# Layer-modulation products of a two-layer diffusion block: from TensorE to a paced VectorE strand

## The chip, the core and the metric

The kernel runs on one core of one Trainium2 chip. The metric is the device time of one execution in microseconds. Five engines matter: TensorE (PE; its weight loads are listed apart as PEld), VectorE (DVE), ScalarE (ACT), GpSimd (POOL), and SyncE (SP), whose queue issues nearly all transfers. Each engine takes its instructions in the order of its own queue, and semaphores make one engine wait for another.

## What is computed

Two layers of a hybrid attention block over 512 latent and 256 context tokens, 2048 wide, in float32. Ahead of each layer a modulation is worked out from two condition vectors (one for the latent stream, one for the context):

```
sc  = silu(c);  scc = silu(c_ctx)
for l in range(2):
    shift, scale, gate       = split(sc  @ w_ada[l] + b_ada[l], 3)
    shift_c, scale_c, gate_c = split(scc @ w_ada[l] + b_ada[l], 3)
    h  = rms(x,  norm_w[l]) * (1 + scale)   + shift
    hc = rms(xc, norm_w[l]) * (1 + scale_c) + shift_c
    ... one input projection (w_in), three kinds of attention (A, B, C), silu gate ...
    x  = x + gate * merge_out(...)            # w_out
    if l == 0: xc = xc + gate_c * merge_out(...)
```

`w_ada[l]` is 2048 x 6144 float32, 48 MB for each layer. Two vectors are multiplied by it, so its reading is large and its arithmetic small. In layer 1 the context's gate is not used, because the context stream ends there.

## The kernel before

The program is written as strands (Python generators) that a planner, the class `Weaver`, interleaves. It keeps a virtual time and a clock for each engine, books an estimated price for each instruction (`bump`), and lets, at each virtual moment, the ready strand with the lowest priority number go on. `gate` holds a strand back while its engine's booked work, or its own data, is more than `AHEAD` = 1.35 us in front of the virtual time. The result is one fixed order for each engine's queue.

The matrix products are exact to float32 by splitting: each weight tile is loaded into a buffer `ws` (3 of them), ScalarE writes its rounded high part to `wh` (3), VectorE writes the remainder to `wl` (2) by the subtraction at line 234, and TensorE multiplies by high and low parts (line 323). One such pair is called a weight piece here; there are 606, in one order, taken in turn by the strand `main` (priority 6) while the strand `splitter` (priority 2) prepares the next. Line 326 holds the transposes, line 228 ScalarE's copies, `S` is the PSUM area of attention scores, `pt` the transposed probabilities. In groups A and B the attention output passes through `ot` to a multiplication on GpSimd (line 277).

The modulation is made by `ada_blocks`, `ada_finish`, `ada_scale` and `ada_gate`. `ada_blocks` takes blocks of columns of `w_ada`. For each it loads the sixteen 128-row tiles; for each of them TensorE uses the 32 columns of `scT` (the two condition vectors and zeros) as weights and streams the 512 (or 256) columns of `w_ada` (line 722) into one of four 32-partition strips of a PSUM bank. `ada_finish` copies the bank to `tm`, sums the strips by small matmuls with the selector `sel` (line 739), which also turns the row to columns, and adds the bias into `ada`.

Layer 0's shift and scale are made at the start, by `ada_scale(0, 256, "s3", ...)`, in blocks of 256 columns. Three parts remain, each in blocks of 512 columns from a ring `wa` of 4 buffers, in groups of four tiles, as bursts with priority 4:

- layer 0's gate (4 blocks, 64 tiles), spawned after attention group B's jobs;
- layer 1's shift and scale (8 blocks, 128 tiles), spawned by layer 0's jobs before group C;
- layer 1's gate (4 blocks, 64 tiles), spawned at the same place in layer 1.

The gates are wanted by `post_out` (it waits for `ev_gate`), when the output projection of their layer begins; shift and scale of layer 1 by `make_h` at the start of layer 1.

Of the kernel before, what the change touches and what calls it, by code (L numbers as in the profile page):

```python
# [18 lines left out]
OP = mybir.AluOpType  # L19
AX = mybir.AxisListType  # L20

D = 2048
# [3 lines left out]
KT = D // 128  # L26
# [13 lines left out]

CUT = [3, 2]

RES = dict(wa=0, s3=8)


def mmc(n):
# [8 lines left out]
class Event:  # L55
# [4 lines left out]
    def __init__(self):  # L60
        self.t = None
# [73 lines left out]
class Kern:  # L135
    def __init__(self, ctx, tc, t):
        self.ctx, self.tc, self.nc, self.t = ctx, tc, tc.nc, t
        self.w = Weaver()
        self.pools, self.avail, self.half = {}, {}, {}
        self.ndram = 0  # L140
        for tag, shape, n in (("s3", (128, 768), 52), ("ws", (128, 512), 3), ("wh", (128, 512), 3),
                              ("wl", (128, 512), 2), ("tm", (128, 512), 5), ("wa", (128, 512), 4),
                              ("pt", (128, 512), 6), ("ot", (128, 256), 2),
                              ("sm", (128, 32), 16)):
            self.pools[tag] = (ctx.enter_context(tc.tile_pool(name=tag, bufs=n)), shape)
            self.avail[tag] = [0.0] * n
        for tag, shape, n in (("g", (128, 512), 6), ("S", (128, 1024), 1)):
            self.pools[tag] = (ctx.enter_context(tc.tile_pool(name=tag, bufs=n, space=bass.MemoryType.PSUM)), shape)
            self.avail[tag] = [0.0] * n
        for tag, n in (("hl", 3), ("hc", 2), ("ck", 3), ("yk", 4), ("rk", 1)):  # L150
            self.avail[tag] = [0.0] * n
        self.static = ctx.enter_context(tc.tile_pool(name="static", bufs=1))
        self.dram = ctx.enter_context(tc.tile_pool(name="scratch", bufs=1, space=bass.MemoryType.DRAM))
# [445 lines left out]
def body(K):  # L599
    nc, t, w = K.nc, K.t, K.w  # L600
# [4 lines left out]
    K.start(ident, t["k_ident"], 65536)  # L605
    flip = K.st([128, 128], name="flip")
    sel = K.st([128, 2], name="sel")
    maskA = K.st([128, 640], BF16, name="maskA")
    maskB = K.st([128, 384], BF16, name="maskB")
    zero = K.st([128, 256], BF16, name="zero")  # L610
    nc.gpsimd.memset(zero, 0.0)
    scT = K.st([128, KT, 32], name="scT")
    nc.vector.memset(scT, 0.0)
    ada = [K.st([128, 48, 2], name=f"ada{l}") for l in range(2)]
    bT = [K.st([128, 48], name=f"bT{l}") for l in range(2)]
# [69 lines left out]
    ev_c, ev_b, ev_go = Event(), Event(), Event()  # L685

    def ada_blocks(l, blocks, stag, ptag, depth, group):
# [6 lines left out]
        for i in range(0, len(items), group):  # L694
# [4 lines left out]
            while len(pend) < group:  # L699
                while nxt < len(items) and len(pend) < depth and K.free(stag) > RES[stag]:  # L700
                    c_, n_, k_ = items[nxt]
# [9 lines left out]
                if len(pend) >= group:  # L711
                    break
                yield lambda: 0.0 if K.free(stag) > RES[stag] else None
            tiles = [pend.popleft() for _ in now]
# [16 lines left out]
    def ada_finish(l, c0, n, ps, ptag):  # L731
        a = yield from K.get("tm")
        yield from K.act(a[:, :n], ps[:, :n])
        K.put(ptag, ps)
        pt = yield from K.get("g")
        yield from K.sync()
        m = n // 128
        for c in range(m):
            nc.tensor.matmul(pt[:, 2 * c:2 * c + 2], a[:, c * 128:(c + 1) * 128], sel, start=c == 0, stop=c == m - 1,  # L739
                             skip_group_check=True)  # L740
        w.pe(0.05 * m)
        f = c0 // 128
        yield from K.wait(ev_b)
        o = ada[l][:, f:f + m, :]
        yield from K.add(o, pt[:, :2 * m].rearrange("p (c m) -> p c m", m=2),
              bT[l][:, f:f + m, None].to_broadcast([128, m, 2]))
        K.put("g", pt)
        K.put("tm", a)
        k0 = f % KT
        if f < KT:  # L750
            ev = ev_sh
        elif f < 2 * KT:
            yield from K.stt(gsc[l][:, k0:k0 + m, :], o, 1.0, nT[l][:, k0:k0 + m, None].to_broadcast([128, m, 2]),
                             OP.add, OP.mult)
            ev = ev_sc
        else:
            ev = ev_gb
        for k in range(k0, k0 + m):
            K.set(ev[l][k])

    def ada_scale(l, n, stag, ptag, depth, group):
        yield from ada_blocks(l, [(c + o, n) for c in range(0, D, n) for o in (0, D)], stag, ptag, depth, group)

    def ada_gate(l, stag, ptag, depth, group):
        yield from ada_blocks(l, [(2 * D + c, 512) for c in range(0, D, 512)], stag, ptag, depth, group)
        yield from K.wait(*ev_gb[l])
        ps = yield from K.get("g")
        yield from K.sync()
        for m in range(2):
            K.tr(ps[:KT, m * 128:(m + 1) * 128], ada[l][:, 32:48, m])  # L770
        w.pe(0.2)
        g = yield from K.get("tm")
        yield from K.act(g[:KT, :256], ps[:KT, :256])
        K.put("g", ps)
        for m in range(2):
            yield from K.store(gscr[l][m], g[:KT, m * 128:(m + 1) * 128], 8192)
        K.put("tm", g)
        K.set(ev_gate[l])
# [452 lines left out]
    def layer(l):  # L1231
# [14 lines left out]
        J = lambda fn: jobs.append(Call(fn))  # L1246
# [183 lines left out]
        ev_c = {(i, s): Event() for i in range(20) for s in ("lat", "ctx") if s == "lat" or i >= 12 or not last}  # L1430
# [407 lines left out]
        for g in range(4):  # L1838
# [3 lines left out]
                jobs.append(zjob(f))  # L1842
            jobs.append(q_job(GB, "B", range(3 * g, 3 * g + 3), (8 + g,)))
            J(lambda g=g: [attend64(GB, "B", h, g, 4 + h // 2) for h in range(3 * g, 3 * g + 3)] and None)
        if l == 0:
            J(lambda: w.spawn(ada_gate(0, "wa", "g", 4, 4), 4))
        for i in (12, 16):
            jobs.append(chunk(GC, "C", [("c", i + j) for j in range(4)], allt))
        jobs.append(FJob(K, W, COL["kpe"], [(0, 384), (384, 768)], rhs_h, ev_h, post_kpe, stack=True))
# [6 lines left out]
        def free_B():  # L1856
            yield lambda: 0.0 if all(e.t is not None for e in ev_y[:10]) else None
            K.put("s3", ropeB["cs"])

        J(lambda: w.spawn(ada_scale(1, 512, "wa", "g", 4, 4) if l == 0 else ada_gate(1, "wa", "g", 4, 4), 4))  # L1860
        for kind, i in ORDER_C:
            if kind == "q":
                jobs.extend(q_jobs(i))
# [32 lines left out]
    def rpb_prep():  # L1896
        yield from K.wait(ev_c)
        K.side(flip, t["k_flip"])
        for l in range(2):
            p = yield from K.get("tm")  # L1900
            nc.gpsimd.memset(p[:120, :64], 0.0)
            K.side(p[:120, 16:47], t["rpb_a"][l].rearrange("h a b -> (h a) b"))
            yield from K.land()
            K.side(rpb_scr[l], p[:120, :64])
            K.put("tm", p)
        for dst, src in ((maskA, t["k_maskA"]), (maskB, t["k_maskB"])):
            p = yield from K.get("s3")
            n = dst.shape[1]
            K.side(p[:, :n], src)
            yield from K.gate("pool")  # L1910
            nc.gpsimd.tensor_copy(dst, p[:, :n])
            w.bump("pool", 0.9)
            K.put("s3", p)
# [7 lines left out]
    def main():  # L1921
        for j in jobs:
            yield from j.run()
        closed[0] = True
# [3 lines left out]
    w.spawn(K.splitter(), 2)  # L1928
    w.spawn(load_x(), 0)
    w.spawn(rpb_prep(), 1)  # L1930
    w.spawn(ada_scale(0, 256, "s3", "g", 10, 2), 3)
    w.spawn(main(), 6)
    w.spawn(worker(), 2)
    w.spawn(worker(), 2)
# [66 lines left out]
```

## Time and profile before

| | us |
|---|---|
| median of 3 runs | 2972.59 (2969.92 to 2973.67) |
| the profiled execution | 2976.81, span 2975.0 |
| PE busy | 2882.8 (97%) |
| PEld busy | 2706.2 (91%) |
| DVE busy | 1758.5 (59%) |
| ACT busy | 1254.2 (42%) |
| POOL busy | 140.1 (5%) |

The profile gives for each engine the time in which an instruction of it ran. TensorE's matmuls are pipelined, so the distance from the start of one group to the start of the next tells what a group takes of the engine's time better than its duration does. The three bursts of modulation lie at 922 to 1160 us (layer 0's gate), 1160 to 1450 us (layer 1's shift and scale) and 2540 to 2710 us (layer 1's gate). Layer 0's attention groups A and B run up to some 1170 us, group C to some 1510 us, the output projection to some 1700 us.

### The profile page before, as it was taken

What the parts mean: (1) busy time and instruction counts of PE and PEld (TensorE: products, weight loads), DVE (VectorE), ACT (ScalarE), POOL (GpSimd) and SP (SyncE); (2) the same over time, 40 slices, a digit from 0 to 9 for tenths busy, and PEclk for the clock granted to TensorE, in tenths of its full rate; (3) what the DMA queues carried; (4) which work ended last, traced back from release to release, by engine and by line L of the source; (5) the groups of instructions that cost most, each with busy time, mean ns of one, the idle gap of its engine ahead of it and who ended that gap; (6) DMA issues with size and microseconds to landing.
All of it is one profiled execution on the core that took longest, in us unless ns stands there. A gap on an engine that the chain in (4) does not pass through costs nothing.

```text
span 2975.0 us, 56930 instructions
## 1 busy us (share of the span) xinstructions
PE 2882.8 (97%) x21819; PEld 2706.2 (91%) x21819; DVE 1758.5 (59%) x4820; ACT 1254.2 (42%) x2730; POOL 140.1 (5%) x189
## 2 busy tenths in 40 slices
PE   5999999999999999999999999999999999999998
PEld 3689999999999899878999989999998999788998
DVE  5345554637757473867634374655677676578643
ACT  4234333425545452545422273443445455346421
POOL 3000000000100010000000000000000000000000
PEclk9999999999999999999999999999999999999999
DMA  9842222221224555547334333333322214543244
GB/s 253 281 136 81 72 78 76 65 70 49 63 60 127 171 145 157 193 150 237 111 111 124 111 104 82 93 96 91 86 73 66 77 59 129 178 156 118 87 154 127
DMA packets 423633, 349.23 MB, mean 117 GB/s; under 512 B 66276, under 2 KB 370210, under 8 KB 423360
## 3 DMA queue, kind: packets, MB, share of 16 engines
q1 hardware_dynamic: 421488, 344.27, 38.7%
q0 software_dynamic: 1872, 1.32, 0.4%
q8 instruction: 171, 2.80, 0.4%
q14 instruction: 102, 0.84, 0.1%
HBM read 303.97 MB, written 32.08 MB: 113 GB/s over the span
## 4 chain that ended last, share of the span: by engine, by line
PE 88%; DVE 5%; DMA 4%; SPq 1%; ACT 1%; issue 1%; DVEq 0%; ACTq 0%
PE g L323 71%; PE S L323 7%; PE g L326 6%; PE g L722 3%; SPq L293 1%; DMA s<-w_ada 1%; DMA s<-scr 1%; ACT s L228 1%; DVE wl L234 1%; DVE s L234 1%; DVE s L267 1%; DVE pt L234 1%; PE g L739 1%; DVE tm L234 0%; DVE s L256 0%
## 5 line engine op out<-in xcount | busy, mean ns | idle before, releaser
L323 PE MATMUL g<-wh,s 128*128 128x256 f32 (+1 forms) x9000 | 1761.5, 289 | 17.1 <-DVE s L234 7.5
L323 PEld LDWEIGHTS g<-wh,s 128*128 128x128 f32 x9000 | 1445.8, 192 | 54.2 <-issue 31.5
L323 PE MATMUL g<-wl,s 128*128 128x256 f32 (+1 forms) x4500 | 1284.5, 285 | 3.0 <-DVE wl L234 3.0
L323 PEld LDWEIGHTS g<-wl,s 128*128 128x128 f32 x4500 | 862.9, 192 | 5.3 <-DVE wl L234 3.9
L234 DVE TENSOR_TENSOR wl<-ws,wh 128x512 fp32r<-128x512 f32 (+1 forms) x598 | 409.7, 686 | 566.2 <-PE g L323 445.9
L228 ACT ACTIVATE wh<-ws 128x512 fp32r<-128x512 f32 (+2 forms) x606 | 372.0, 615 | 471.8 <-PE g L323 428.2
L323 PE MATMUL g<-s,wh 128*128 128x384 f32 (+1 forms) x1664 | 465.2, 356 | 0.9 <-ACT tm L228 0.9
L228 ACT ACTIVATE s<-s,sm 128x640 f32<-128x640 f32 (+3 forms) x260 | 195.8, 753 | 379.9 <-DVE sm L267 295.4
L323 PEld LDWEIGHTS g<-s,wh 128*128 128x128 f32 x1664 | 304.4, 188 | 21.1 <-ACT tm L228 1.1
L323 PE MATMUL g<-s,wl 128*128 128x384 f32 (+1 forms) x768 | 271.7, 354 | 0.0
L228 ACT ACTIVATE tm<-g 128x512 f32<-128x512 f32 (+4 forms) x324 | 160.7, 517 | 247.6 <-PE g L323 147.5
L234 DVE TENSOR_TENSOR pt<-g,pt 128x512 fp32r<-128x512 f32 (+1 forms) x338 | 196.4, 591 | 92.3 <-ACT pt L228 91.1
L323 PE MATMUL S<-s,s 128*128 128x256 f32 (+2 forms) x1260 | 238.8, 318 | 6.5 <-DVE sm L267 6.1
L326 PE MATMUL g<-ident,s 128*128 128x128 f32 x1520 | 232.7, 277 | 9.8 <-DVE s L234 6.1
L228 ACT ACTIVATE pt<-g 128x512 fp32r<-128x512 f32 (+1 forms) x338 | 168.7, 516 | 155.6 <-PE g L326 149.9
L323 PE MATMUL g<-pt,s 128*128 128x256 f32 (+1 forms) x1348 | 216.7, 286 | 7.4 <-DVE pt L234 4.8
L323 PEld LDWEIGHTS S<-s,s 128*128 128x128 f32 x1260 | 187.2, 190 | 28.6 <-DVE sm L267 12.1
L326 PEld LDWEIGHTS g<-ident,s 128*128 128x128 f32 x1520 | 177.3, 142 | 36.1 <-issue 12.6
L323 PEld LDWEIGHTS g<-pt,s 128*128 128x128 f32 x1348 | 186.5, 192 | 17.6 <-DVE pt L234 7.2
L277 POOL TENSOR_TENSOR s<-ot,s 64x256 f32<-64x256 f32 x100 | 79.3, 794 | 1922.2 <-DVE ot L234 1905.9
L323 PEld LDWEIGHTS g<-s,wl 128*128 128x128 f32 x768 | 144.7, 188 | 9.7 <-DVE wl L234 0.2
L251 DVE TENSOR_SCALAR s<-s,sm 128x640 f32<-128x640 f32 (+3 forms) x260 | 131.8, 507 | 6.1
(146 smaller groups left out, 2129.9 us busy)
## 6 DMA issues: line engine op xcount, KB each, us to landing
wa<-w_ada SPq DMA_DIRECT2D x256, 256.0 KB
ws<-w_in SPq DMA_DIRECT2D x328, 128.0 KB
ws<-w_in SPq DMA_DIRECT2D x160, 256.0 KB
ws<-w_out SPq DMA_DIRECT2D x136, 256.0 KB
s<-w_ada SPq DMA_DIRECT2D x128, 256.0 KB
s<-scr SPq DMA_DIRECT2D x36, 384.0 KB
ws<-w_in SPq DMA_DIRECT2D x64, 192.0 KB
ws<-w_qb SPq DMA_DIRECT2D x54, 192.0 KB
```

The costliest lines, as they stand in the source:

```text
L228: self.nc.scalar.activation(out, in_, func, bias=bias, scale=scale, **kw)
L234: self.nc.vector.tensor_tensor(out, a, b, op=op)
L251: self.nc.vector.tensor_scalar(out, a, s1, s2, op0=op0, op1=op1)
L267: self.nc.vector.tensor_tensor_reduce(out, a, b, -1.0, init, OP.add, OP.min, acc)
L277: self.nc.gpsimd.tensor_tensor(out, a, b, op=OP.mult)
L293: self.nc.sync.dma_start(out, in_)
L323: self.nc.tensor.matmul(out, l, r, start=start, stop=stop, skip_group_check=True)
L326: self.nc.tensor.transpose(out, in_, self.ident)
L722: nc.tensor.matmul(ps[j:j + 32, :n], scT[:, kk, :], s[:, x * n:(x + 1) * n], start=kk < 4, stop=kk >= 12, skip_group_check=True)
L739: nc.tensor.matmul(pt[:, 2 * c:2 * c + 2], a[:, c * 128:(c + 1) * 128], sel, start=c == 0, stop=c == m - 1, skip_group_check=True)
```

## The change

Everything behind layer 0's shift and scale is moved from the bursts to one strand, `ada_rest`, with priority 5, spawned when layer 0's shift and scale are done: layer 0's gate, then layer 1's shift and scale, then layer 1's gate. In it, `ada_vec` keeps one accumulator of 128 x 512 for each side (latent, context) in the new pool `ac` (2 buffers; `wa` goes from 4 to 2). For each tile of `w_ada` VectorE multiplies by the tile's column of `scT` and adds into the accumulator: `tensor_scalar` for the first tile of a block, `scalar_tensor_tensor` for the other fifteen. After each tile the strand is held until 4.0 us (`PACE`) of virtual time later. When a block is complete, TensorE sums the accumulator over the partitions by four matmuls for each side with a column of ones (`one`). Layer 1's gate is made for the latent side alone. The selector matmuls of layer 0's shift and scale are booked at 0.21 us instead of 0.05.

```diff
-RES = dict(wa=0, s3=8)
+RES = dict(s3=8)
+PACE = 4.0
...
-("wa", (128, 512), 4),
+("wa", (128, 512), 2), ("ac", (128, 512), 2),
...
+    one = K.st([128, 1], name="one")
+    nc.vector.memset(one, 1.0)
...
-        w.pe(0.05 * m)
+        w.pe(0.21 * m)
+        K.put("tm", a)
+        yield from ada_use(l, c0, n, pt, (0, 1))
+
+    def ada_vec(l, c0s, sides):
+        n = 512
+        items = [(c0, k) for c0 in c0s for k in range(KT)]
+        pend = deque()
+        nxt = 0
+        for c0 in c0s:
+            acc = []
+            for k in range(KT):
+                while nxt < len(items) and (not pend or K.free("wa")):
+                    w.cur.ft = w.vt
+                    s = yield from K.get("wa")
+                    c_, k_ = items[nxt]
+                    nxt += 1
+                    ts = yield from K.load_ahead(s, t["w_ada"][l, k_ * 128:(k_ + 1) * 128, c_:c_ + n])
+                    pend.append((s, ts))
+                s, ts = pend.popleft()
+                yield from K.wait(ev_c)
+                w.cur.ft = max(w.vt, ts)
+                if k == 0:
+                    for _ in sides:
+                        acc.append((yield from K.get("ac")))
+                for a, m in zip(acc, sides):
+                    sc = scT[:, k, m:m + 1]
+                    if k == 0:
+                        yield from K.ts(a, s, sc, OP.mult, fast=True)
+                    else:
+                        yield from K.stt(a, s, sc, a, OP.mult, OP.add)
+                K.put("wa", s)
+                yield w.vt + PACE
+            pt = yield from K.get("g")
+            yield from K.sync()
+            for c in range(n // 128):
+                for a, m in zip(acc, sides):
+                    nc.tensor.matmul(pt[:, 2 * c + m:2 * c + m + 1], a[:, c * 128:(c + 1) * 128], one,
...
+            w.pe(0.21 * n // 128 * len(sides))
+            K.put("ac", *acc)
+            w.spawn(ada_use(l, c0, n, pt, sides), 1, w.cur.ft)
...
-    def ada_gate(l, stag, ptag, depth, group):
-        yield from ada_blocks(l, [(2 * D + c, 512) for c in range(0, D, 512)], stag, ptag, depth, group)
+    def ada_gate(l):
+        sides = (0, 1) if l == 0 else (0,)
+        yield from ada_vec(l, [2 * D + c for c in range(0, D, 512)], sides)
...
-        if l == 0:
-            J(lambda: w.spawn(ada_gate(0, "wa", "g", 4, 4), 4))
...
-        J(lambda: w.spawn(ada_scale(1, 512, "wa", "g", 4, 4) if l == 0 else ada_gate(1, "wa", "g", 4, 4), 4))
...
-    w.spawn(ada_scale(0, 256, "s3", "g", 10, 2), 3)
+    def modulation():
+        yield from ada_scale(0, 256, "s3", "g", 10, 2)
+        w.spawn(ada_rest(), 5)
+
+    def ada_rest():
+        yield from ada_gate(0)
+        yield from ada_vec(1, [c + o for c in range(0, D, 512) for o in (0, D)], (0, 1))
+        yield from ada_gate(1)
+
+    w.spawn(modulation(), 3)
```

Because the planner orders everything anew, the change moves instructions on all engines. In the listings that follow, a row is a line, an operation, its output and inputs; the kernel's lines shift by two in the changed one (234 becomes 236, 256 becomes 258, 323 becomes 325).

TensorE's queue in attention group B of layer 0, kernel before: the first burst's first group of four tiles (`wa,scT`) stands between products with probabilities (`pt`) and the next scores (`S`).

```order
L323 MATMUL g<-pt,s_9235 128x256 x4
L323 MATMUL g<-pt,s_9235 128x128 x2
L722 MATMUL g<-wa,scT 32x512 x4
L323 MATMUL S<-s_9231,s_10412 128x256
L323 MATMUL S<-s_9232,s_10412 128x256
```

In the changed kernel no such group stands between them. TensorE's queue in attention group A of layer 0, changed kernel: the sum of the first block's two accumulators (`ac`) over the partitions, in the midst of a product of the input projection.

```order
L325 MATMUL g<-s_1264,wl 128x384
L325 MATMUL g<-s_1265,wh 128x384
L784 MATMUL g<-one,ac 128x1 x8
L325 MATMUL g<-s_1032,wh 128x384
L325 MATMUL g<-s_1032,wl 128x384
```

On TensorE 64 groups of four rows at line 722 and 64 matmuls at line 739 are gone, and 112 matmuls of one column have come.

VectorE's queue from the 128th weight piece to the 129th (`wl<-ws,wh`), in attention group B of layer 0, kernel before (`ISA` rows are the maxima and the reads of their accumulators, `ot` the attention's output).

```order
L234 TENSOR_TENSOR wl<-ws,wh 128x512
L234 TENSOR_TENSOR sm<-sm 128x1
L272 RECIPROCAL sm<-sm 128x1
L251 TENSOR_SCALAR s_10729<-s_10729,sm 128x640
L267 ISA s_10688,sm<-S,maskB,nsink 128x384
L267 ISA sm 128x1
L234 TENSOR_TENSOR s_10413<-g,s_10413 64x512
L267 ISA s_10688,sm<-S,zero,sm 128x256
L267 ISA sm 128x1
L234 TENSOR_TENSOR pt<-g,pt 128x512
L234 TENSOR_TENSOR sm<-sm 128x1
L234 TENSOR_TENSOR wl<-ws,wh 128x512
```

Everything between the two subtractions belongs to attention. The same stretch of VectorE's queue, the 128th weight piece to the 129th, in the changed kernel.

```order
L236 TENSOR_TENSOR wl<-ws,wh 128x512
L253 TENSOR_SCALAR s_10181<-s_10181,sm 128x512
L258 SCALAR_TENSOR_TENSOR s_9819<-g,colA,s_9818 64x256
L236 TENSOR_TENSOR ot<-g,ot 64x256
L258 SCALAR_TENSOR_TENSOR ac<-wa,scT,ac 128x512 x2
L269 ISA s_10362,sm<-S,zero,nsink 128x256
L269 ISA sm 128x1
L236 TENSOR_TENSOR pt<-g,pt 128x512 x2
L236 TENSOR_TENSOR sm<-sm 128x1
L236 TENSOR_TENSOR wl<-ws,wh 128x512
```

Two accumulations stand between two subtractions that TensorE's weights need, and the attention's work around them is that of another head.

SyncE's queue where the first burst's tiles are issued, kernel before: four tiles of `w_ada` together between weight loads.

```order
L293 DMA ws<-w_in 128x2x256 x4
L293 DMA wa<-w_ada 128x512 x4
L293 DMA ws<-w_in 128x2x256 x2
L293 DMA wa<-w_ada 128x512 x4
L293 DMA ws<-w_in 128x2x256
L293 DMA wa<-w_ada 128x512 x4
```

The changed kernel has no groups of four. SyncE's queue in the changed kernel, in attention group B of layer 0.

```order
L295 DMA wa<-w_ada 128x512
L295 DMA ws<-w_in 128x2x192
L295 DMA ws<-w_in 128x2x64
L295 DMA scr_146<-s_5988 128x768
L295 DMA wa<-w_ada 128x512
L295 DMA ws<-w_in 128x2x192
L295 DMA ws<-w_in 128x2x64
```

The 256 loads of `wa` remain, singly spread from layer 0's group A to its output projection.

## Rows read from the trace of the kernel before

**Rows 1.** The page: busy time by engine, and the chain that ended last by engine.
```profile
PE 2882.8 (97%) x21819; PEld 2706.2 (91%) x21819; DVE 1758.5 (59%) x4820; ACT 1254.2 (42%) x2730; POOL 140.1 (5%) x189
...
PE 88%; DVE 5%; DMA 4%; SPq 1%; ACT 1%; issue 1%; DVEq 0%; ACTq 0%
```

**Rows 2.** Timeline of PE at two places: start us, duration us, engine, line, operation.
```profile
921.82 0.89 PE L323 MATMUL g<-pt,s 128*128 128x256 f32 x6
922.64 1.06 PE L722 MATMUL g<-wa,scT 128*32 128x512 f32 x8
923.63 0.51 PE L323 MATMUL S<-s,s 128*128 128x256 f32 x2
...
953.13 1.05 PE L739 MATMUL g<-sel,tm 128*128 128x2 f32 x8
954.04 0.41 PE L326 MATMUL g<-ident,tm 128*128 128x128 f32 x2
```

**Rows 3.** Timeline of PEld at the first place; in brackets idle time before, and releaser.
```profile
922.63 0.16 PEld L722 LDWEIGHTS g<-wa,scT 128*32 128x32 f32 x8
923.63 0.30 PEld L323 LDWEIGHTS S<-s,s 128*128 128x128 f32 x2 [0.84 <-issue]
```

**Rows 4.** Busy time of each engine in three stretches, columns in the first line.
```profile
core 0: us, PE busy (x) PEld busy (x) DVE busy (x) ACT busy (x) POOL busy (x), PEclk, DMA share, GB/s
203.00:1170.00 967.00, 960.51 (x7241) 936.65 (x7239) 564.38 (x1657) 411.22 (x946) 66.04 (x86) 1.00 0.32 90
1170.00:1511.00 341.00, 332.99 (x2435) 288.43 (x2436) 240.00 (x689) 169.41 (x378) 4.34 (x7) 0.99 0.52 171
2540.00:2710.00 170.00, 164.48 (x1098) 137.61 (x1097) 114.16 (x310) 81.57 (x190) 0.00 (x0) 1.00 0.50 160
```

**Rows 5.** PE and PEld busy time of lines 722 and 739 in the bursts, summed.
```profile
sum 700.00, PE 75.81 PEld 11.82; mean PE 25.27 PEld 3.94
...
sum 1478.00, PE 15.31 PEld 15.86; mean PE 5.10 PEld 5.29
```

**Rows 6.** VectorE's groups by form: count, busy us, mean ns of one, idle before.
```profile
L256 DVE SCALAR_TENSOR_TENSOR s<-s,qaT,s 128x512 fp32r<-128x512 f32 x6 | 4.4, 748 | 1.0 <-ACT s L228 1.0
L256 DVE SCALAR_TENSOR_TENSOR s<-tm,g 128x512 f32<-128x512 f32 x16 | 10.9, 683 | 1.0 <-ACT tm L228 0.2
L251 DVE TENSOR_SCALAR s<-s,gsc,ada 128x512 f32<-128x512 f32 x16 | 8.7, 543 | 0.3
L234 DVE TENSOR_TENSOR wl<-ws,wh 128x512 fp32r<-128x512 f32 x544 | 380.0, 699 | 544.5 <-PE g L323 427.7 <-issue 60.5 <-ACT wh L228 29.9
```

**Rows 7.** What VectorE waits for at `wl`, 203 to 1170 us and 1170 to 1511 us.
```profile
DVE wl L234 <- PE g L323: 139.5, 60, 5.4
...
DVE wl L234 <- PE g L323: 9.4, 8, 3.6
```

**Rows 8.** Seven stretches of 50 us with VectorE fullest: last, and sum.
```profile
2700.00:2750.00 50.00, 48.81 (x379) 47.10 (x378) 44.55 (x123) 33.85 (x81) 0.00 (x0) 1.00 0.31 103
sum 350.00, PE 344.98 PEld 320.53 DVE 287.36 ACT 194.95 POOL 23.59; mean PE 49.28 PEld 45.79 DVE 41.05 ACT 27.85 POOL 3.37
```

**Rows 9.** What PE's weight loads at line 722 wait for, 920 to 2710 us.
```profile
PEld g L722 <- issue: 6.4, 30, 0.3
PEld g L722 <- DMA wa<-w_ada: 5.5, 11, 1.0
PEld g L722 <- DVE s L256: 0.7, 1, 0.7
```

**Rows 10.** Timeline of DVE and of POOL around 278 us.
```profile
277.80 1.24 DVE L234 TENSOR_TENSOR wl<-ws,wh 128x512 fp32r<-128x512 f32 x1
...
277.76 0.73 POOL L277 TENSOR_TENSOR s<-ot,s 64x256 f32<-64x256 f32 x1 [29.55 <-DVE ot L234]
```

**Rows 11.** What SyncE's queue waits for before it issues, the longest entry.
```profile
SPq L293 <- DVE wl L234: 1103.6, 374, 12.0
```

More of the change, by code (lines that the diff above doesn't have):

```diff
@@ L141, in __init__ @@
         for tag, shape, n in (("s3", (128, 768), 52), ("ws", (128, 512), 3), ("wh", (128, 512), 3),
-                              ("wl", (128, 512), 2), ("tm", (128, 512), 5), ("wa", (128, 512), 4),
+                              ("wl", (128, 512), 2), ("tm", (128, 512), 5), ("wa", (128, 512), 2), ("ac", (128, 512), 2),
                               ("pt", (128, 512), 6), ("ot", (128, 256), 2),
@@ L740, in ada_finish @@
                              skip_group_check=True)
-        w.pe(0.05 * m)
+        w.pe(0.21 * m)
[35 more added lines that the diff above has]
+                    nc.tensor.matmul(pt[:, 2 * c + m:2 * c + m + 1], a[:, c * 128:(c + 1) * 128], one,
+                                     start=c == 0 and m == sides[0], stop=c == n // 128 - 1 and m == sides[-1],
+                                     skip_group_check=True)
+            w.pe(0.21 * n // 128 * len(sides))
+            K.put("ac", *acc)
+            w.spawn(ada_use(l, c0, n, pt, sides), 1, w.cur.ft)
@@ L742, in ada_finish, with ada_use @@
+    def ada_use(l, c0, n, pt, sides):
+        m = n // 128
         f = c0 // 128
         yield from K.wait(ev_b)
-        o = ada[l][:, f:f + m, :]
-        yield from K.add(o, pt[:, :2 * m].rearrange("p (c m) -> p c m", m=2),
-              bT[l][:, f:f + m, None].to_broadcast([128, m, 2]))
+        x, y = sides[0], sides[-1] + 1
+        o = ada[l][:, f:f + m, x:y]
+        yield from K.add(o, pt[:, :2 * m].rearrange("p (c m) -> p c m", m=2)[:, :, x:y],
+              bT[l][:, f:f + m, None].to_broadcast([128, m, y - x]))
@@ L747, in ada_finish @@
         K.put("g", pt)
-        K.put("tm", a)
         k0 = f % KT
@@ L768, in ada_gate @@
         yield from K.sync()
-        for m in range(2):
+        for m in sides:
             K.tr(ps[:KT, m * 128:(m + 1) * 128], ada[l][:, 32:48, m])
@@ L772, in ada_gate @@
         g = yield from K.get("tm")
-        yield from K.act(g[:KT, :256], ps[:KT, :256])
+        yield from K.act(g[:KT, :128 * len(sides)], ps[:KT, :128 * len(sides)])
         K.put("g", ps)
-        for m in range(2):
+        for m in sides:
             yield from K.store(gscr[l][m], g[:KT, m * 128:(m + 1) * 128], 8192)
```

## The prediction

> **What bounds the kernel now.** I read busy times and chain first: TensorE is busy 97% of the span and holds 88% of the chain, VectorE is busy 59% and holds 5% of the chain [rows 1]. So TensorE's own work sets the time, and an instruction taken off it is worth what it keeps the next one from starting. Then I read the timeline at a modulation group: the eight records of four tiles (each matmul of this float32 kind has two) start at 922.64 and the next product at 923.63 [rows 2]; the reader is to look at starts, since the printed durations overlap. Last I read the stretches in which the new VectorE work will stand: attention groups A and B of layer 0, 203 to 1170 us, with VectorE busy 564.38 of 967 and TensorE idle 6.5; group C of layer 0, 1170 to 1511 us, with VectorE busy 240.00 of 341 and TensorE idle 8.0 [rows 4]. They tell whether there is room.
>
> The profiled execution took 2976.81 us (span 2975.0 and 1.8 around it), 4.2 above the median of the three runs, 2972.59. The sum below is made against 2976.8, and 4.2 is taken off at the end.
>
> **What TensorE loses and gains.** Removed: 64 groups of four tiles at 923.63 - 922.64 = 0.99 us, 63.4 us. All of it is path, since in both places the engine goes straight on with other work. The busy time of line 722, 75.81 us [rows 5], is the upper end; it counts tails that overlap. Removed too: 64 selector matmuls. Four of them, eight records, take 954.04 - 953.13 = 0.91 us [rows 2], 0.228 each, 14.6 us. Added: 112 matmuls with the column of ones (32 for layer 0's gate, 64 for layer 1's shift and scale, 16 for layer 1's gate), with the same 128 x 128 weights as the selector's, so 0.228 each, 25.5 us. Net: 63.4 + 14.6 - 25.5 = **52.5 us less** on TensorE. The copies of banks by ScalarE and a 16-row transpose that also go are off the path or under 1 us, and I cost them at nothing, as ScalarE is busy 42% [rows 1].
>
> TensorE's waits at the bursts go as well: 5.5 us for tiles, 0.7 for VectorE, 6.4 of issue [rows 9]. Between 0 and 12.6 us; some of that time becomes another wait, since the instruction behind would often not have been ready earlier. I take 4.
>
> **What VectorE gets.** 28 tensor-scalar of 128 x 512 and 420 scalar-tensor-tensor of 128 x 512. The nearest row for the first is 543 ns. For the second there are 748 ns (two SBUF inputs and a per-partition scalar, the same shape, six times) and 683 ns (one input in PSUM) [rows 6]; I take 748, which has the same operands. 28 x 0.543 + 420 x 0.748 = 329 us (302 by 683 ns). VectorE then stands at some 1758.5 + 329 = 2088 us, about 71% of a shorter span.
>
> Where they stand I read from the order, with the 606 weight pieces as a common clock: of the 448, 11 are in front of piece 20, 352 between pieces 20 and 200 (203 to 1170 us in the trace), 64 between 200 and 260 (1170 to 1511 us), 21 behind.
> - Groups A and B: 564 + 352 x 0.748 = 827 us of work in a stretch that stays near 967 us on TensorE (16 groups of tiles and 16 selector matmuls go, -19.5 us; some 11 sums of 1.82 come, +20): 85%. There is slack of the right kind: VectorE stands 139.5 us there waiting for TensorE to free a weight buffer [rows 7], that is, it is early. What does 85% cost TensorE? In the seven 50 us stretches of the trace with the fullest VectorE (41.05 of 50 on average) TensorE is idle 50 - 49.28 = 0.72 us [rows 8], against 6.5/967 x 50 = 0.34 here. 967/50 x 0.38 = 7.3; I take **+8 us**, with 0 and 16 as ends (1.19 in the fullest stretch).
> - Group C: 240 + 64 x 0.748 = 288 us of work. TensorE's own time falls by 32 groups and 32 selector matmuls, 39 us, and two sums come, 4 us: 341 - 35 = 306 us. VectorE would stand at 94%, more than any 50 us of the trace shows (44.55, 89% [rows 8]). And it is early there for only 9.4 us [rows 7]: most of its gaps wait for ScalarE's half of softmax. At 89% the stretch needs 288/0.89 = 323 us, so 17 of the 35 us are given back; at 94% none. I take **+12**.
>
> Such an added instruction also waits for its tile at the head of VectorE's queue, and behind it stand the subtractions for `wl`, for which TensorE waits two pieces later. The ring has only two buffers, but the tile is issued about one tile ahead, and the 4 us of pacing is far over the 0.99 us that four tiles took of TensorE. The 256 loads are the same in number and size; the 16 DMA engines are busy 32% at 203 to 1170 us with 90 GB/s [rows 4], and 176 loads of 256 kB there instead of 64 add some 30 GB/s, which keeps them under half. SyncE's queue now meets a load of `wa` that waits for VectorE between weight loads; but it already waits 1103.6 us for `wl` subtractions in total [rows 11], which means that weights are issued as early as buffers allow. Cost nothing while VectorE keeps up; if it doesn't, that is rival 1.
>
> A wider VectorE share also meets GpSimd. A 128 x 512 subtraction that began 0.04 us after a GpSimd multiplication took 1.24 us, against 0.699 on average [rows 10, 6]. 93 GpSimd operations stand between 203 and 1511 us; with the added work filling 27% of that time, some 25 meet one, 25 x 0.55 = 14 us more of VectorE time and 1 point of its share, inside the ends above. The Trainium skill, "SBUF — State Buffer", section "SBUF: two separate sides", says that a VectorE operation with two SBUF inputs and a GpSimd operation exclude each other for the whole of an instruction; the trace agrees (1.24 us is 0.69 and most of the other's 0.73), and by that rule alone the added work would lose these 14 us, not more.
>
> Behind piece 300 nothing is added. In layer 1 the gate's burst goes: 16 groups, 4 sums of 0.91 for 4 of as much, -16 us, already in the 52.5. VectorE is busy 114.16 of 170 there [rows 4], so it can follow.
>
> **Sum.** 2976.8 - 52.5 - 4 + 8 + 12 = 2940.3 for a profiled execution, less 4.2: **2936 us**, 1.2% less.
>
> **Rival 1, slower: VectorE's queue becomes what TensorE waits for.** Place: groups A to C of layer 0. Each added operation stands in front of softmax and of subtractions in an engine that takes its queue in order; where VectorE is behind the plan, the whole of it is delay for TensorE, and the `wa` load in SyncE's queue holds the weights behind it. It decides from 56.5/329 = 17% of the added time on the path. For it: group C's 94%, and that the planner books 0.60 us for a subtraction that takes 0.699 [rows 6], so it sees free time that isn't there. Against it: 0.72 us idle at 82% [rows 8]. With a third of the added time on the path, 329/3 = 110 us: 2976.8 - 56.5 + 110 - 4.2 = **3026 us**. Chance 0.14.
>
> **Rival 2: full giving back in group C and in the fullest part of group B.** VectorE at no more than 82% on average, what the seven fullest stretches show [rows 8]: group C needs 288/0.82 = 351 us against 306, +45, and A and B 827/0.82 = 1009 against 967, +42. Then 2976.8 - 56.5 + 87 - 4.2 = 3003; with group C alone 2976.8 - 56.5 + 8 + 45 - 4.2 = **2969**, within 0.2% of before. Chance of about that: 0.10.
>
> **Rival 3: TensorE is bound by its weight loads, not by what streams.** Then removing groups with small weights frees only 11.82 us and the selectors' 15.86 [rows 5], and the sums cost 224 records x 15.86/128 = 27.8: nothing is gained, and with +20 for VectorE the time is 2972.6 + 20 = 2993. Against it: behind the group's loads PEld stands idle 0.84 us, and the next load starts with the next product at 923.63 [rows 3]; the streaming holds everything. Chance 0.02. The Trainium skill, "Perfetto Trace Analysis", section "Identifying the Most-Contended Engine", wants TensorE judged by LDWEIGHTS busy share and not by matmul busy time; here the row on PEld speaks against taking it so.
>
> That the change does not do what it says: the last accumulation of layer 0's gate stands, by the order, where the trace has some 520 us and `post_out` asks at 1511; layer 1's scale stands at some 1250 us and is asked for at 1690. No wait can arise there, and I give it nothing.
>
> **How the numbers follow.** My forecast has 0.74, rival 1 0.14, rival 2 0.10, rival 3 0.02. The forecast's own range: the low end takes all waits and none of VectorE's costs, 2976.8 - 52.5 - 12.6 - 4.2 = 2908; the high end takes 16 and 17 and no waits, 2953. Holding 8 in 10 it must take in rival 2, and the first part of rival 1 (where it decides, 2973 and a little over), so 2908 to 2980. About 0.2%, 6 us, is what a measurement of this kernel can tell from no change. Faster by more than that (under 2966.6): 0.74 and a part of rival 2, 0.75. Within: 0.10. Slower: 0.15.
>
> **What would show it.** Right: no line 722 behind 200 us; TensorE's busy time down by 50 to 60 us; VectorE's up by 300 to 340 with the accumulation near 0.75 us; the waits of `wl` for TensorE in groups A and B shorter by about as much as the added work; group C's stretch shorter by 15 to 35 us, layer 1's last 400 us by some 16. Wrong: accumulations of 0.9 us or more, TensorE idle by over 1.5 us in 50 in groups A and B, weight loads (PEld) waiting for `wl`, or SyncE's queue waiting for accumulations while `ws` is wanted.

## The result and the profile after

The changed kernel takes 2958.74 us (median of 4 runs, 2956.14 to 2960.64), the kernel before, measured beside it, 2973.13. The ratio is 0.9949, with a 95% interval of 0.9932 to 0.9967: 0.5% faster, some 15 us, where 36.5 were forecast. The direction was right, the size was not half of it. A repeat on another chip gave 0.9946 (below).

The page of the changed kernel, busy time by engine and the chain that ended last, to be held against [rows 1]:

```profile
PE 2835.2 (96%) x21402; PEld 2716.2 (92%) x21402; DVE 2025.2 (69%) x5269; ACT 1243.4 (42%) x2714; POOL 147.3 (5%) x189
...
PE 77%; DVE 13%; DMA 5%; issue 2%; SPq 2%; ACT 1%; DVEq 0%; ACTq 0%
```

TensorE lost 47.6 us of busy time, near the forecast, but the chain tells that VectorE now holds 13% of what ended last instead of 5%. The span fell by 20.6 in the profiled execution, which is the fastest of its four runs; the medians are 14.4 apart.

With the weight pieces as common clock (VectorE's subtractions for `wl` or `wh` numbers 20, 200 and 260, counted from 0, start at 200, 1189 and 1509 us now, at 203, 1170 and 1511 before) the stretches of the changed kernel are, in the columns of [rows 4]:

```profile
0.00:200.00 200.00, 158.75 (x1333) 119.35 (x1334) 95.20 (x229) 71.60 (x140) 25.57 (x44) 0.99 0.84 249
200.00:1189.00 989.00, 971.05 (x7264) 957.09 (x7264) 783.95 (x2021) 410.44 (x945) 74.03 (x86) 0.99 0.41 117
1189.00:1509.00 320.00, 295.67 (x2146) 280.22 (x2145) 269.31 (x746) 163.10 (x371) 4.28 (x7) 0.99 0.39 122
1509.00:2954.00 1445.00, 1409.76 (x10665) 1359.53 (x10663) 876.75 (x2276) 598.26 (x1260) 43.43 (x52) 0.99 0.35 100
```

| stretch (pieces) | before, us | after, us | difference | forecast |
|---|---|---|---|---|
| start (to 20) | 203 | 200 | -3 | 0 |
| groups A and B of layer 0 (20 to 200) | 967 | 989 | +22 | +8.5 |
| group C of layer 0 (200 to 260) | 341 | 320 | -21 | -23 |
| behind it | 1464 | 1445 | -19 | -16 |

The forecast's column holds 30.5 of its 36.5 us: the 4 us of waits were placed in no stretch, and 2 us of small matmuls behind group C were not counted (see the section on why the prediction was wrong). The profiled execution took 2956.14 us where the sum had 2940.3 for it. So most of the 15.8 us that are missing, 13.5, lie in groups A and B. There TensorE's idle time went from 6.5 us [rows 4] to 989 - 971.05 = 17.95. The rest is the clock. Two stretches of 50 us in groups A and B and two in group C, changed kernel, same columns:

```profile
550.00:600.00 50.00, 45.26 (x307) 43.47 (x307) 42.82 (x124) 22.26 (x55) 3.57 (x5) 0.97 0.33 96
750.00:800.00 50.00, 40.58 (x258) 35.71 (x258) 44.72 (x122) 26.98 (x70) 5.13 (x6) 0.86 0.26 78
1250.00:1300.00 50.00, 41.67 (x283) 37.30 (x282) 43.91 (x128) 24.56 (x56) 0.00 (x0) 0.97 0.25 81
1350.00:1400.00 50.00, 47.94 (x353) 46.76 (x352) 45.84 (x152) 30.86 (x74) 1.06 (x2) 0.97 0.46 139
```

The kernel before had VectorE at 39.84 of 50 in its own 750 to 800 us, and lost nothing of the clock there:

```profile
750.00:800.00 50.00, 47.91 (x319) 46.46 (x319) 39.84 (x131) 27.02 (x73) 5.28 (x7) 1.00 0.25 66
```

From 750 to 800 us TensorE now stands for 9.4 us, and the granted clock averages 0.86 of 2.4 GHz, that is, 14 us of the 50 at the level of 1.2 GHz. With 0.97 from 550 to 600 us the clock cost (0.14 + 0.03) x 50 = 8.5 us. So groups A and B: 11.5 of idle time + 8.5 of clock + 0.5 of added matmuls = 20.5 of the 22.

The last row of the table hides a loss. The output projection of layer 0, before and then changed:

```profile
1511.00:1688.00 177.00, 172.88 (x1440) 172.53 (x1439) 68.07 (x115) 35.44 (x55) 0.00 (x0) 1.00 0.37 114
...
1509.00:1692.00 183.00, 177.38 (x1455) 176.76 (x1454) 81.48 (x138) 35.13 (x56) 0.00 (x0) 0.98 0.47 141
```

It takes 6 us more, with a granted clock of 0.98 instead of 1.00 and 1.5 us more of idle time. The stretch of layer 1's gate takes 23 less (below).

What TensorE waits for from 500 to 1000 us (engine, line, releaser: us in total, times, longest), and an excerpt of its timeline there:

```profile
PE g L328 <- DVE s L253: 5.9, 7, 1.6
PE g L325 <- DVE pt L236: 3.7, 8, 0.8
PE S L325 <- DVE sm L269: 3.1, 7, 0.6
```

```profile
776.42 0.74 PE L325 MATMUL S<-s,s 128*128 128x256 f32 x4 [0.54 <-DVE sm L269]
777.00 0.28 PE L328 MATMUL g<-ident,s 128*128 128x128 f32 x1
778.36 0.90 PE L328 MATMUL g<-ident,s 128*128 128x128 f32 x3 [1.08 <-DVE s L253]
779.90 1.44 PE L325 MATMUL S<-s,s 128*128 128x384 f32 x4 [0.64 <-DVE sm L269]
...
786.49 0.90 PE L328 MATMUL g<-ident,s 128*128 128x128 f32 x3 [1.62 <-DVE s L253]
```

The waits are for softmax: the maximum (line 269), the scaling of the probabilities ahead of their transposes (253), the second half of the transposed probabilities (236). The weight subtraction, which the prediction had named beside softmax, is not among them here. In group C it is the longest entry, for matmuls as for weight loads (1180 to 1500 us):

```profile
PE g L325 <- DVE wl L236: 5.9, 8, 1.9
...
PEld g L325 <- DVE wl L236: 9.0, 11, 2.1
```

And most of the slack I counted on is gone: in groups A and B VectorE waited 139.5 us at `wl` for TensorE [rows 7], now 20.4. Another 68.4 us in front of `wl` (16.2 before) are put down to no engine:

```profile
DVE wl L236 <- issue: 68.4, 48, 3.4
DVE wl L236 <- PE g L325: 20.4, 19, 2.9
```

The added operations by form (count, busy us, mean ns):

```profile
L258 DVE SCALAR_TENSOR_TENSOR ac<-wa,scT,ac 128x512 f32<-128x512 f32 x420 | 308.9, 755 | 9.4 <-DMA wa<-w_ada 8.7
L251 DVE TENSOR_SCALAR ac<-wa,scT 128x512 f32<-128x512 f32 x28 | 13.1, 480 | 5.5 <-DMA wa<-w_ada 4.4 <-PE g L784 1.1
```

### The profile page after: what moved, and what is told of

Its sections match the earlier page's. It is cut to its first block, busy times and chain, and to the rows that moved or that the text cites. A ratio compares the mean times of both kernels' runs of the same rounds, so it can differ in the third digit from the quotient of the medians.

```text
span 2954.4 us, 56418 instructions
## 1 busy us (share of the span) xinstructions
PE 2835.2 (96%) x21402; PEld 2716.2 (92%) x21402; DVE 2025.2 (69%) x5269; ACT 1243.4 (42%) x2714; POOL 147.3 (5%) x189
## 4 chain that ended last, share of the span: by engine, by line
PE 77%; DVE 13%; DMA 5%; issue 2%; SPq 2%; ACT 1%; DVEq 0%; ACTq 0%
PE g L325 65%; PE g L328 5%; PE S L325 5%; DVE s L236 2%; DVE s L269 2%; DVE wl L236 2%; DVE ac L258 2%; SPq L295 2%; DMA s<-w_ada 1%; DMA s<-scr 1%; DVE pt L236 1%; DVE tm L236 1%; DVE s L253 1%; ACT s L230 1%; DVE s L258 1%
## 5 line engine op out<-in xcount | busy, mean ns | idle before, releaser
L258 DVE SCALAR_TENSOR_TENSOR ac<-wa,scT,ac 128x512 f32<-128x512 f32 x420 | 308.9, 755 | 9.4 <-DMA wa<-w_ada 8.7
L230 ACT ACTIVATE tm<-g 128x512 f32<-128x512 f32 (+3 forms) x308 | 150.9, 512 | 247.5 <-PE g L325 139.2
L325 PE MATMUL g<-pt,s 128*128 128x256 f32 (+1 forms) x1348 | 223.8, 290 | 14.9 <-DVE pt L236 8.8
L325 PEld LDWEIGHTS S<-s,s 128*128 128x128 f32 x1260 | 189.3, 192 | 26.2 <-DVE sm L269 15.8
L279 POOL TENSOR_TENSOR s<-ot,s 64x256 f32<-64x256 f32 x100 | 86.7, 867 | 1934.9 <-DVE ot L236 1714.9
```

Of the source, the lines that this page charges most:

```text
L230: self.nc.scalar.activation(out, in_, func, bias=bias, scale=scale, **kw)
L258: self.nc.vector.scalar_tensor_tensor(out, a, s, b, op0=op0, op1=op1)
L279: self.nc.gpsimd.tensor_tensor(out, a, b, op=OP.mult)
L325: self.nc.tensor.matmul(out, l, r, start=start, stop=stop, skip_group_check=True)
```

## The experiments

Two theories at the start. **V**: VectorE's added time takes the gain, through TensorE's waits for softmax and the clock lost behind them. **O**: it is not the time but what came with it, the new order of all queues or the 256 single loads in SyncE's queue.

**The changed kernel again**, on another chip.

> The changed kernel as it is, on the chip of the other runs of this set: 2956 to 2962 us, so that the distances to it rest on the same chip.

Measured 2958.09 us, ratio 0.9946 (0.9934 to 0.9958).

**VectorE's time taken away, order kept.**

```diff
-yield from K.stt(a, s, sc, a, OP.mult, OP.add)
+yield from K.gate("dve")
+nc.vector.scalar_tensor_tensor(a[:, :32], s[:, :32], sc, a[:, :32], op0=OP.mult, op1=OP.add)
+w.bump("dve", 0.07 + 0.06 + 0.00104 * n)
```

> The changed kernel with its order, loads, sums and booked prices untouched, but each of the 420 accumulations works on 32 of its 512 columns (so the modulation behind layer 0's shift and scale is only partly computed). This takes VectorE's time away and nothing else. Theory V (VectorE's added time is what ate the gain, by TensorE's waits and the clock lost behind them): the accumulation falls from 755 ns to about 0.25 us, some 210 us of VectorE time go, and nearly the whole expected gain appears: 2916 us, between 2905 and 2925. Rival O (the new order itself, or the single loads in SyncE's queue): nothing moves, 2950 to 2960.

Measured 2936.69 us, ratio 0.9869 (0.9856 to 0.9883): between the two. The accumulation fell to 256 ns, 209 us of VectorE time went, and 22 us of the kernel's time with it. Some 21 were still missing to the 2916 us of the sum. Every queue had the same order as in the changed kernel, so these can't be VectorE's added time, beyond what the narrow accumulations still take. Its accumulations, and its stretches (pieces 20 to 200, 200 to 260, and behind):

```profile
L778 DVE SCALAR_TENSOR_TENSOR ac<-wa,scT,ac 128x32 f32<-128x32 f32 x420 | 99.9, 256 | 7.5 <-DMA wa<-w_ada 6.8
...
203.00:1178.00 975.00, 964.37 (x7267) 954.51 (x7266) 629.92 (x2021) 410.80 (x946) 65.94 (x86) 0.99 0.41 119
1178.00:1493.00 315.00, 296.32 (x2146) 284.01 (x2146) 241.75 (x747) 162.82 (x371) 4.32 (x7) 0.97 0.40 125
1493.00:2938.00 1445.00, 1409.22 (x10666) 1358.19 (x10665) 865.02 (x2276) 597.63 (x1260) 43.70 (x52) 0.99 0.34 100
```

In group C TensorE still stands for 18.7 us, with hardly more VectorE work than before (241.75 us against 240.00 [rows 4]). So V is true in part, and O in part.

**The same, with nothing booked for the accumulations**, which orders the other work as if they did not exist.

```diff
-w.bump("dve", 0.07 + 0.06 + 0.00104 * n)
+w.bump("dve", 0.0)
```

> As e1_narrow (accumulations on 32 of 512 columns, the modulation behind layer 0's shift and scale only partly computed), and the planner books nothing for them, so that the other work is ordered as if they didn't exist. It tells apart the two reasons why e1_narrow stayed 21 us over what the sum allows. Theory P (the booked load made the planner delay attention's work, and the order carries that): 2913 to 2925 us. Theory F (TensorE's bursts had stood where TensorE would wait anyway, above all in group C, so that taking them out is worth less than their length): 2928 to 2940 us, with TensorE idle over 12 us in pieces 220 to 260.

Measured 2910.31 us, ratio 0.9786 (0.9773 to 0.9799). That is some 64 us, more than the 56.5 I had summed for TensorE, and a little under the range of theory P; in a new order theory F is out. The 256 single loads, the sums on TensorE and 113 us of VectorE work are all in it. So no cost of the loads shows; what was left of theory O is the order that booking the accumulations gave. By the stretches of the two kernels it cost 7 us in groups A and B, 12 in group C (TensorE idle 18.7 us instead of 9.4) and 8 behind it:

```profile
202.00:1170.00 968.00, 960.33 (x7273) 951.12 (x7271) 633.83 (x2048) 409.87 (x942) 65.83 (x86) 1.00 0.43 124
1170.00:1473.00 303.00, 293.64 (x2150) 283.08 (x2151) 240.45 (x739) 162.85 (x373) 4.28 (x7) 0.98 0.42 133
1473.00:2910.00 1437.00, 1404.97 (x10649) 1354.04 (x10648) 861.69 (x2253) 597.72 (x1259) 44.05 (x52) 0.99 0.34 97
```

**The fourth corner: nothing booked, but the accumulations done in full.**

> The full accumulations, but booked at nothing: the order of e5_free on every engine, with VectorE's real time in it. The fourth corner of the square (booked or not, done or not). If the two costs add, order 26 us (e1_narrow less e5_free) and VectorE's real time 22 us (the changed kernel less e1_narrow): 2932 us, 2927 to 2938. If the booking is what keeps VectorE's real time harmless, that is, unplanned work does more harm than planned work: 2945 us or more.

Measured 2972.21 us, ratio 0.9997 (0.9986 to 1.0008). The costs don't add. In this order VectorE's real time (757 ns for an accumulation, against 264) costs 62 us, three times what it costs in the booked order. Its groups A and B:

```profile
202.00:1217.00 1015.00, 978.86 (x7273) 958.65 (x7272) 800.26 (x2048) 409.48 (x942) 74.91 (x86) 0.99 0.41 118
```

VectorE is busy 79% of it, as in the changed kernel (783.95 of 989); TensorE is idle 36.1 us instead of 17.95. The square, by ratios to the kernel before:

| | accumulations of 32 columns | of 512 columns |
|---|---|---|
| booked | 0.9869 | 0.9949 |
| not booked | 0.9786 | 0.9997 |

By these ratios booking costs 25 us of order when VectorE is light, and saves 14 when it is not. What it is in the booked order that TensorE loses to is not shown.

**What a group on TensorE is worth in a fixed order.** Kernel before, every queue as it was, three of four groups in each block narrowed.

```diff
-nc.tensor.matmul(ps[j:j + 32, :n], scT[:, kk, :], s[:, x * n:(x + 1) * n], start=kk < 4, stop=kk >= 12,
+m = 32 if stag == "wa" and kk >= 4 else n
+nc.tensor.matmul(ps[j:j + 32, :m], scT[:, kk, :], s[:, x * n:x * n + m], start=kk < 4, stop=kk >= 12,
```

> The kernel before, order and booked prices untouched, but in the bursts the matmuls of the second to fourth group of each block stream 32 of 512 columns (the modulation behind layer 0's shift and scale is only partly computed). 48 of the 64 groups shrink from 0.99 us to an estimated 0.25. No VectorE work, no new order. If the whole length of a group is path, as my sum has it: 35 us less, 2940 us (2935 to 2945), half of it in pieces 200 to 260. Theory F: pieces 200 to 260 give less than 9 us of their 18, the two gates their 9 each, in all 2948 to 2956 us.

Measured 2954.53 us, ratio 0.9932 (0.9919 to 0.9946), some 20 us, as theory F has it in all. A narrowed group takes 0.20 us from start to start, so 48 x 0.79 = 38 us were taken away (9.5 for each gate, 19 in group C). Timeline of PE at two of them:

```profile
928.10 0.27 PE L723 MATMUL g<-wa,scT 128*32 128x32 f32 x8
928.30 0.74 PE L323 MATMUL S<-s,s 128*128 128x256 f32 x4
...
935.71 0.27 PE L723 MATMUL g<-wa,scT 128*32 128x32 f32 x8
936.42 0.86 PE L323 MATMUL S<-s,s 128*128 128x384 f32 x4 [0.44 <-DVE sm L267]
```

At the second the next product was not ready, and 0.44 us go into a wait for VectorE. Its stretches:

```profile
199.00:1163.00 964.00, 954.17 (x7246) 937.82 (x7246) 565.11 (x1658) 410.98 (x946) 65.98 (x86) 1.00 0.32 90
1163.00:1496.00 333.00, 319.24 (x2436) 293.83 (x2435) 238.69 (x688) 168.40 (x378) 4.34 (x7) 0.98 0.53 176
1496.00:2958.00 1462.00, 1426.53 (x10813) 1368.25 (x10811) 864.83 (x2257) 599.87 (x1264) 43.44 (x52) 0.99 0.36 106
```

The gains are 3, 8 and 2 us. So theory F, which gave the gates their whole 9 us each and the loss to group C alone, has the total but not the place. This profiled execution is the slowest of the five, and in it some 21 of the 38 us came back: TensorE's idle time is 101.2 us instead of 92.2, and its granted clock 0.990 instead of 0.994 on average, 12 us over 2958. In a fixed order about half of what leaves TensorE is given back in this way; with a new order, as above, nothing is.

**Sparser pace.** PACE 5.0 and 6.0 for 4.0.

> The changed kernel with PACE 5.0 instead of 4.0: pieces 20 to 200 hold 286 added operations instead of 353, and some 40 move to layer 1, where VectorE has room. Theory V: the fuller stretches of groups A and B lose less, 2945 to 2953 us. Rival O: no change beyond 3 us, 2956 to 2962, or slower if the last parts come late.

> The changed kernel with PACE 6.0: 246 operations instead of 353 in pieces 20 to 200, layer 1's shift and scale complete only as layer 0 ends. Theory V: 4 to 8 us better than PACE 5.0 up to piece 260, 2940 to 2946, unless layer 1's start waits for the last blocks: then pieces 300 to 320 are longer by 5 us or more, and the whole is 2946 to 2955.

Measured 2947.02 us, ratio 0.9908 (0.9895 to 0.9922), and **2930.06 us, ratio 0.9854 (0.9841 to 0.9868)**: the direction of theory V, with more at the second step than its 2940 to 2946. How much of that is VectorE's time, the next runs tell. PACE 6.0 is the fastest complete kernel of this study, faster than the kernel before and the changed one. Pieces 20 to 200 of it:

```profile
205.00:1164.00 959.00, 953.62 (x7211) 945.14 (x7210) 718.80 (x1913) 411.26 (x944) 70.82 (x86) 1.00 0.37 107
```

VectorE at 75%, TensorE idle 5.4 us, no clock lost: 30 us less than the changed kernel needs there.

**PACE 6.0 without booking, and PACE 6.0 with narrow accumulations.**

> The full accumulations, booked at nothing, PACE 6.0. If both remedies add (sparser pace takes 28 us off the booked kernel, about two thirds of what booking and real time cost together): 2918 to 2926 us, better than each alone. If unplanned work does harm: 2935 or more, worse than PACE 6.0 with booking (2930).

> PACE 6.0 with booking, accumulations on 32 of 512 columns (the modulation behind layer 0's shift and scale only partly computed): what VectorE's real time costs at the sparser pace. If the cost grows with how full VectorE is, much less than the 22 us at PACE 4.0: 2920 to 2928, 2 to 10 under PACE 6.0 with full accumulations. If it goes with the number of operations alone, which is the same: 2908, 22 under.

Measured 2973.41 us, ratio 0.9994 (0.9986 to 1.0003), and 2919.11 us, ratio 0.9813 (0.9798 to 0.9828). Without booking nothing is gained at the sparser pace either. Pieces 20 to 200 of that kernel:

```profile
202.00:1199.00 997.00, 967.68 (x7218) 950.63 (x7218) 739.04 (x1938) 407.72 (x942) 74.72 (x86) 1.00 0.37 106
```

VectorE is busy 74% here, the share of the kernel above, and TensorE idle 29.3 us instead of 5.4. So the share of VectorE alone does not set the cost. With booking, VectorE's real time costs 11 us at this pace (2930.06 less 2919.11), half of the 22 at PACE 4.0, for the same number of operations; the run came out an us under the range of the theory that the cost grows with how full VectorE is. The two kernels with narrow accumulations differ too, 2936.69 and 2919.11, or 17 us by their ratios. So of the 28 us that the sparser pace brought, some 11 are VectorE's time, and the larger part is the order that came with it: theory O as much as V.

**Parts of the change.** Layer 1's gate alone on VectorE; then both gates, with layer 1's shift and scale left on TensorE. The rest, with the selectors' booked price, is as in the kernel before.

```diff
+if l == 1:
+    J(lambda: w.spawn(ada_gate(1), 5))
```

> One part of the change alone: only layer 1's gate (latent side, 64 tiles) goes to VectorE, spread from the start of layer 1; layer 0's gate and layer 1's shift and scale stay as bursts on TensorE, as before. By the two traces all of the measured gain comes from this part, because layer 0 comes out even. Theory V: 16 groups and their waits go, 64 operations of 0.75 us meet a VectorE that is 65% busy: 2950 to 2956 us, the same as the whole change or a little better. If instead the parts help each other (layer 0's changes pay later), this alone gives less than 8 us: 2965 or more.

> Both gates on VectorE, sparsely (a tile each 12 us in layer 0, each 8 us in layer 1), layer 1's shift and scale left as bursts on TensorE in group C, as before (accumulators and ring share five buffers). Theory V and F together: 32 groups leave TensorE where it is full, 192 operations of 0.75 us spread over 1600 us cost next to nothing, and group C keeps its filling: 2940 to 2948 us, at least 8 better than layer 1's gate alone. If a VectorE operation costs TensorE the same wherever it stands (some 0.04 us each, as in the changed kernel): 2945 to 2952.

Measured 2954.32 us, ratio 0.9930 (0.9917 to 0.9944), and 2947.77 us, ratio 0.9914 (0.9901 to 0.9926). Layer 1's gate alone, a seventh of the added operations, brings as much as the whole change or a little more. The stretch around it in the kernel before and in the changed one:

```profile
2522.00:2715.00 193.00, 187.48 (x1220) 157.53 (x1218) 123.94 (x331) 88.10 (x201) 0.00 (x0) 1.00 0.49 154
...
2525.00:2695.00 170.00, 162.23 (x1033) 150.00 (x1032) 119.25 (x321) 85.30 (x194) 0.00 (x0) 0.99 0.25 74
```

That is 23 us for work of 16. With this gate alone on VectorE everything behind group C takes 1441 us instead of 1464, the same 23, and the two stretches ahead of it are as before (968 and 340). Both gates came out at the upper end of what V expects and inside what the other theory expects, and 6.5 us better than layer 1's gate alone, 5 by the ratios, not the 8 that V and F wanted; so this run does not tell the theories apart. In its profile groups A and B take 958 us instead of 967, but everything behind group C 1449, 8 more than with layer 1's gate alone; the granted clock from 1501 to 1690 us is 0.96 there.

**The planner's prices.** I had held that the planner sees free VectorE time that isn't there, since it books 0.60 us for 0.699.

```diff
-self.w.bump("dve", 0.07 + 0.00104 * self.n(out))
+self.w.bump("dve", 0.15 + 0.00104 * self.n(out))
```

(and the like for VectorE's other operations, tensor-scalar at 0.00052 per column)

> The changed kernel with the planner's prices for VectorE set to what the trace shows (a fixed term of 0.15 us instead of 0.07 for all, tensor-scalar at 0.52 ns per column). The instructions are the same, the order is new: pieces 20 to 200 hold 298 added operations instead of 353. Theory V with its sub-claim (the planner sees free VectorE time that isn't there): 2940 to 2950 us. If the planner's prices are not the matter: 2955 to 2965.

Measured 2968.81 us, ratio 0.9977 (0.9966 to 0.9987): some 10 us worse than the changed kernel. So prices nearer the trace do not bring the gain back; one new order can't tell whether the planner's errors cost nothing. Where this order loses (groups A and B 985 us, everything behind group C 1466 us instead of 1445) is seen, why is not settled.

## Why the prediction was wrong

- **TensorE's own part, 52.5 us and 4 of waits: right in size, wrong as a reason.** Busy time fell by 47.6, and the order without booking and with little VectorE work gives 64. But "all of it is path" was read from starts in the trace. In the fixed order about half of 38 us came back as waits and lost clock. The sum was reached only with a new order.
- **What VectorE's work costs: the term that failed.** The sum has 8 + 12 = 20 us. Between the kernel with narrow, unbooked accumulations and the changed kernel lie 48 (2958.74 less 2910.31): 22 go with VectorE's real time in the order of the changed kernel, the rest is the order that planning for it gave. (In the unbooked order its real time alone costs 62, so the split holds for this order.) The sum had no term for a new order, and none for the clock.
- **Groups A and B: the step where it failed.** I put +8 for VectorE at 85%, taken from the seven fullest 50 us stretches of the trace before [rows 8]. It became +22: 11.5 of idle time and 8.5 of clock. By the stretches 14 of the 22 go with VectorE's real time (989 to 975 us with narrow accumulations) and 7 with the order (975 to 968 unbooked). VectorE's share was even lower than forecast (79%, since instructions overlap in the records: 322 us of added operations raised the busy time by 267; I had gone by starts for TensorE and by durations for VectorE). The idle time of the seven stretches was no price for added work; that they were full of work in an order made for them is my reading and not shown. The runs show the same share at 5.4 and at 29.3 us of idle time (74 to 75%), and at 18 and 36 (79%).
- **Group C: right in sum (-23 forecast, -21), in part by luck.** TensorE's idle time there rose by 24.3 - 8.0 = 16.3 us, near the 12 to 17 of the forecast. But the reason was to be a VectorE at 89% or more, and it stood at 84% (269.31 of 320). With narrow accumulations the stretch still takes 315 us, and 303 in the order without booking: 5 us go with VectorE's time, 12 with the order.
- **Layer 1's gate: right** (-16 forecast, -23 in its stretch), VectorE has room. The output projection of layer 0, for which I had nothing, takes 6 us back.
- **Rival 1** had the mechanism (VectorE's queue). Of its places, softmax held TensorE in groups A and B, the weight subtractions in group C; the price was nearer the forecast than the rival's 110 us. **Rival 2** expected the giving back in group C, 351 us with VectorE at 82%; it took 320 at 84%. **Rival 3** is refuted: narrowing what streams, with every weight load left in place, brought 20 us. The Trainium skill, "Perfetto Trace Analysis", section "Identifying the Most-Contended Engine", judges how near TensorE is to its limit by the share of peak arithmetic (MFU) and by LDWEIGHTS busy share, and not by matmul busy time. As a price for the groups their LDWEIGHTS time, 11.82 us [rows 5], would have been too low; here the matmul's start-to-start time was the better guide.
- **The signs.** Of the signs of being right, TensorE's busy time (-47.6 for 50 to 60) and VectorE's (+267 for 300 to 340) fell just short, and the waits at `wl` for TensorE shrank by 119 us where some 250 of accumulations came. Of the signs of being wrong two came: TensorE idle by 4.7 and 9.4 us of 50 in two stretches of groups A and B, and weight loads waiting for `wl` in group C. SyncE's queue waited 53.0 us for accumulations; whether `ws` was wanted meanwhile is not shown.
- **Two slips in the working**, of 2 us or less. The added work fills 24% of 203 to 1511 us (416 x 0.748 of 1308), not 27%. And two of the four sums for layer 1's gate stand in front of the end of group C by the prediction's own counts, so 2 us more should go behind it.
- **The 4.2 us taken off** for the profiled execution of before went the other way in after, whose profiled run was the fastest of four (2.6 under its median). These 6.8 us and the 15.8 of the profiled execution make up the gap of 22.7.

## What to carry to other kernels

Work moved from the bound engine to a half-idle one is not priced by that engine's share alone. It costs where the bound engine's next instruction stands behind it, and where it makes a planner order the rest in another way. Measure the one by running the moved work at a fraction of its size in the same order, the other by leaving it out of the plan. Where a planner fixes the order, try such work spread more thinly; here a third less per microsecond took 28 us off, and planning the full work without booking its time lost everything. And add a term for the clock whenever new short waits come in clusters.

## What the runs showed of the hardware

- TensorE went to its 1.2 GHz level behind a cluster of short waits. From 765 to 777.4 us of the changed kernel it was busy 7.71 of 12.4 us, its longest wait 1.43 us, at a granted clock of 1.00. From 777.6 to 791 us, busy 9.84 of 13.4 us, the granted clock was 0.50, and behind that, with no idle time, 0.99:

```profile
767.40 0.38 PE L325 MATMUL g<-pt,s 128*128 128x256 f32 x1 [1.43 <-ACT pt L230]
...
765.00:777.40 12.40, 7.71 (x48) 5.80 (x46) 10.89 (x30) 6.09 (x18) 0.72 (x1) 1.00 0.30 90
777.60:791.00 13.40, 9.84 (x34) 7.76 (x35) 11.36 (x35) 5.38 (x13) 1.48 (x2) 0.50 0.12 40
791.00:800.00 9.00, 9.00 (x69) 9.00 (x69) 7.79 (x20) 6.12 (x19) 0.73 (x1) 0.99 0.16 43
```

- Sixteen times fewer columns make an accumulation only three times shorter: 755 ns for 512, 256 to 264 ns for 32.
- GpSimd's 64 x 256 multiplication went from 794 ns on average (page of before) to 867 with the accumulations beside it, and back to 789 with accumulations of 32 columns. The Trainium skill, "SBUF — State Buffer", section "SBUF: two separate sides", says that a VectorE operation with two SBUF inputs and a GpSimd operation that reads SBUF exclude each other; the runs agree, at 73 ns on average over 100 multiplications.
